# A mixture-of-experts scatter-add that takes the gather's index and bound instead of a row of its own for slots without a token

## The chip, the cores and the metric

The program runs on one core of one Trainium2 chip. The metric is the device time of one execution in microseconds, from the first to the last instruction of that core, lower is better. One launch computes the whole reference; nothing is computed on the host.

## The reference, cut to what matters

The reference is three stages on 512 tokens of width 1024: two hybrid layers (a gated delta rule, attention, a linear recurrence), one layer with differential attention and retention, and at the end of that layer a mixture of experts with 64 experts of which each token uses 8. Only this last part is touched. Cut to its core it is:

```python
scores = sigmoid(h @ router_w)                       # (512, 64)
top_e  = top 8 of the 4 best of 8 groups             # (512, 8)
wts    = scores[top_e] / sum * 2.5
tok_buf = full((n_pad,), t).at[dest].set(t_s)        # slots of experts; an empty slot names row t
h_pad   = concatenate([h, zeros((1, d))])
def body(acc, (tok, wt, e)):                         # blocks of 128 slots of one expert
    xb = h_pad[tok]
    yb = (silu(xb @ w1[e]) * (xb @ w3[e])) @ w2[e]   # 1024 -> 256 -> 1024
    return acc.at[tok].add(yb * wt[:, None])
out = rmsnorm(x + g2 * (acc[:t] + shared(h)))
```

512 tokens with 8 experts each are 4,096 pairs of a token and an expert.

## The kernel before

**Who sets the order.** The kernel does not issue instructions as it is written. Every engine operation is first recorded (`Rec.add`), and a list scheduler (`Rec.plan`) then sorts the whole program, from the first layer to the last expert, by estimated durations and priorities (the longest path to the end). Line 411 issues everything, so all instructions carry that line in the profile, and groups are told apart by tile names. A recorded operation that is left out shifts the ranks of what follows, and the scheduler may then place other operations elsewhere. PE, DVE, ACT, POOL and SP each run their own list strictly in order.

**The mixture of experts** (`block3`). `h2` makes the normalised rows and writes them to a DRAM tensor `h2d`; it also copies the residual into the accumulator `accd` in DRAM. `route` finds for each expert which slot each token takes, and sorts the experts by their number of tokens; the sorted experts get slots by a fixed table:

```python
FIXED = 4
CAPS = (96,) * 4 + (192,) * 4 + (128,) * 5 + (96,) * 11 + (80,) * 11 + (64,) * 7 + (48,) * 14 + (32,) * 8
```

The sum of this table is 5,104 slots for the 4,096 pairs; with the given inputs every expert fits, so 1,008 slots hold no token, and a loop for what overflows (line 2276) runs no iteration. The four experts with 192 slots ("wide experts") are worked off in two blocks, of 128 and of 64 slots; all others are one block. That makes 68 blocks. With these inputs the wide experts hold 183, 145, 132 and 130 tokens, and the last two experts 16 and 12 tokens in 32 slots each.

**One block** (`block`, then `ffn`) does this for its `c` slots:
1. DVE makes a one-hot matrix `oh` (tokens by slots), PE multiplies it with the table `aux` (in the profile a matmul `ps<-aux,b`), DVE sums the result into `m`: the token's number less a large constant `HUGE`, and the weight.
2. DVE turns it into an index, `ix`: with `HUGE` added back a slot with a token has the token's row, a slot without one has 1,048,576.
3. POOL issues a gather (`DMA_INDIRECT raw<-h2d,m`) of `c` rows of 4 KB into the buffer `X`, with a bound: rows past 511 are skipped.
4. PE transposes `X` (eight `ps<-const,raw`), ACT and DVE split half of the result into two fp32r parts, PE multiplies with the expert's weights (`ps<-raw,b` for the quarter in plain fp32, `ps<-b,b` for the rest).
5. DVE scales the result into the buffer `Y` (`SCALAR_TENSOR_TENSOR raw<-ps,m,b`), and POOL issues a scatter (`DMA_INDIRECT accd<-raw,m`) that adds its `c` rows to `accd`. In this kernel the scatter has no bound. Its own index column holds `min(ix, 512 + slot)`: the accumulator has 128 extra rows, set to zero in `shared`, and a slot without a token adds to one of them.

`X` lies in three buffers (`raw4` to `raw6`). `Y` shares four (`raw0` to `raw3`) with the first sixth of each expert's weights, which SP loads (`raw<-in_ew_dram`); SP loads the rest into smaller buffers `b`. A scatter waits for the scatter before it (both write `accd`), and POOL's list is one queue, in which scatters and gathers alternate. The shared expert (`shared`) adds its 512 rows with four more scatters. After the last scatter `tail` reads `accd`, normalises and writes the output.

Of the kernel before, what the change touches and what calls it, by code (L numbers as in the profile page):

```python
# [12 lines left out]
F32 = mybir.dt.float32  # L13
F32R = mybir.dt.float32r
BF16 = mybir.dt.bfloat16
I32 = mybir.dt.int32
U32 = mybir.dt.uint32
AF = mybir.ActivationFunctionType
OP = mybir.AluOpType
AX = mybir.AxisListType  # L20

T = 512
NT = 4
D = 1024
# [1380 lines left out]
HUGE = 1048576.0  # L1405
# [455 lines left out]
class K3(K2):  # L1861
    def h2(self):
        nc = self.nc
        self.acc = self.dr.tile([640, D], F32, name="accd")
        self.h2d = self.dr.tile([T, D], F32, name="h2d")
        G = [self.mrow(4, i) for i in range(2)]
        S = [self.mrow(3, i) for i in range(2)]
        hs = []
        for t in range(NT):
            r = self.rstd1(self.x[t], "h2")  # L1870
            for i in range(2):
                x = self.x[t][i]
                nc.sync.dma_start(self.acc[t * 128:(t + 1) * 128, i * 512:(i + 1) * 512], x)
                nc.vector.scalar_tensor_tensor(x, x, r, G[i], op0=OP.mult, op1=OP.mult)
                o = self.t2()
                pk = lambda a: a.rearrange("q (p k) -> q p k", k=4)
                nc.vector.tensor_tensor(out=o.rearrange("q (k p) -> q p k", k=4), in0=pk(x), in1=pk(S[i]), op=OP.add)
                nc.sync.dma_start(self.h2d[t * 128:(t + 1) * 128, i * 512:(i + 1) * 512], o)
                hs.append(o)
        self.h = []  # L1880
        for k in range(8):
            p = self.psum("tr")
            for t in range(NT):
                self.tr(p[:, t * 128:(t + 1) * 128], hs[2 * t + k // 4][:, (k % 4) * 128:(k % 4 + 1) * 128])
            hi, lo = self.t2(F32R), self.t2(F32R)
            self.split(p, hi, lo)
            self.h.append((hi, lo))

    def route(self):
        nc, A = self.nc, self.A  # L1890
        C = lambda w, n, dt=F32: self.cst.tile([128, w], dt, name=n)
# [73 lines left out]
        ipart, cap, dcap = self.c2[:, 385:386], self.c2[:, 450:451], self.c2[:, 451:452]  # L1965
# [45 lines left out]
        for i in range(3):  # L2011
            d = self.aux[:, :, :, 3 + i]
            nc.vector.tensor_copy(d, s3(rem))
            if i < 2:
                nr = self.t2()[:, :256]
                nc.vector.tensor_tensor(out=s3(nr), in0=s3(rem), in1=d, op=OP.subtract)
                rem = nr
        self.dump_row = C(1, "dumprow")
        nc.vector.tensor_scalar(self.dump_row, ipart, 512.0, None, op0=OP.add)
        pc = self.psum("a")  # L2020
        for t in range(4):
            nc.tensor.matmul(pc[0:64, 0:1], mb[:, 64 * t:64 * t + 64], onesb[:, 0:1], start=(t == 0), stop=(t == 3))
# [35 lines left out]
    def shared(self):  # L2058
        nc, A = self.nc, self.A
        self.g2 = [nc.keep(self.mrow(5, i)) for i in range(2)]  # L2060
        at4 = self.small(4, "at4", I32)
        for t in range(NT):
            nc.vector.tensor_scalar(at4[:, t:t + 1], self.c2[:, 385:386], 128.0 * t, None, op0=OP.add)
        z = self.t2()
        nc.gpsimd.memset(z, 0.0)
        for i in range(2):
            nc.sync.dma_start(self.acc[512:640, i * 512:(i + 1) * 512], z)
        ph = {(i, j): self.psum("mm") for i in range(2) for j in range(2)}
        at = []
        for h in range(2):  # L2070
            for i, n in enumerate(("shared_w1", "shared_w3")):
                nc.gate = at[-SHAHEAD] if len(at) >= SHAHEAD else self.mark - GATE[2]
                w = self.load_w(A[n].rearrange("(h p k) f -> p h k f", h=2, k=4)[:, h], tags=(SHRAW,) + SHTAG)
                nc.gate = None
                at.append(len(nc.ops))
                for k in range(4):
                    hh, hl = self.h[4 * h + k]
                    for j in range(2):
                        wh, wl = (x[:, 128 * j:128 * j + 128] for x in w[k])
                        for q, (a, b) in enumerate(((wh, hh), (wl, hh), (wh, hl))):  # L2080
                            nc.tensor.matmul(ph[i, j], a, b, start=(h + k + q == 0), stop=(h + k + q == 6))
        nc.gate = at[-SHAHEAD2]
        w2 = [self.load_w(A["shared_w2"][j * 128:(j + 1) * 128].rearrange("p (k d) -> p k d", k=2), tags=(SHRAW,) + SHTAG)
              for j in range(2)]
        nc.gate = None
        hs = []
        for j in range(2):
            th, ac, ha = (self.t2() for _ in range(3))
            nc.scalar.activation(th, ph[0, j], AF.Tanh, scale=0.5)
            nc.vector.scalar_tensor_tensor(ac, th, 1.0, ph[0, j], op0=OP.add, op1=OP.mult)  # L2090
            nc.vector.tensor_tensor(out=ha, in0=ac, in1=ph[1, j], op=OP.mult)
            hh, hl = self.t2(F32R), self.t2(F32R)
            nc.scalar.activation(hh, ha, AF.Copy, scale=0.5)
            nc.vector.scalar_tensor_tensor(hl, ha, 0.5, hh.bitcast(F32), op0=OP.mult, op1=OP.subtract)
            hs.append((hh, hl))
        for t in range(NT):
            s = slice(t * 128, (t + 1) * 128)
            y = self.t2(tag=YTAG)
            for n in range(2):
                py = self.psum("mm")  # L2100
                self.mm3(py, [((hs[j][0][:, s], hs[j][1][:, s]), w2[j][n]) for j in range(2)])
                yn = y[:, 512 * n:512 * n + 512]
                nc.scalar.activation(yn, py, AF.Copy)
                nc.gpsimd.tensor_tensor(out=yn, in0=yn, in1=self.g2[n], op=OP.mult)
            nc.gpsimd.indirect_dma_start(out=self.acc[:], out_offset=Ind(at4[:, t:t + 1]), in_=y, in_offset=None,
                                         compute_op=OP.add)
            yield 9.0
# [72 lines left out]
    def block(self, w, pos, aux, c=128):  # L2180
        nc = self.nc
# [5 lines left out]
        for t in range(4):  # L2187
            nc.tensor.matmul(pm, oh[:, t, :], aux(t), start=(t == 0), stop=(t == 3))
        m = self.small(2, "m")[:c]
        nc.vector.tensor_reduce(m, pm.rearrange("p (a b) -> p a b", a=2), axis=AX.X, op=OP.add)  # L2190
        ix = self.small(2, "ix", I32)[:c]
        nc.vector.tensor_scalar(ix[:, 0:1], m[:, 0:1], HUGE, None, op0=OP.add)
        nc.vector.tensor_scalar(ix[:, 1:2], m[:, 0:1], HUGE, self.dump_row[:c], op0=OP.add, op1=OP.min)
        xs = []
        X = self.t2(tag="wr")[:c]
        nc.gpsimd.indirect_dma_start(out=X, out_offset=None, in_=self.h2d[:], in_offset=Ind(ix[:, 0:1]),
                                     bounds_check=T - 1, oob_is_err=False)
        for h in range(2):
            px = self.psum("a")[:, :4 * c]
# [13 lines left out]
        Y = self.t2(tag=YTAG)[:c]  # L2213
        for n in range(2):
            nc.vector.scalar_tensor_tensor(Y[:, 512 * n:512 * n + 512], ys[n], m[:, 1:2], self.g2[n][:c], op0=OP.mult, op1=OP.mult)
        nc.gpsimd.indirect_dma_start(out=self.acc[:], out_offset=Ind(ix[:, 1:2]), in_=Y, in_offset=None, compute_op=OP.add)

    def hold(self, q):
        self.nc.gate = self.seen.get(q, self.mark)
# [144 lines left out]
```

## Time and profile before

| what | value |
|---|---|
| time, median of 3 runs | 2389.94 us (2387.89 to 2395.32) |
| the profiled execution's own time | 2396.73 us |
| its span, first to last instruction | 2395.0 us |
| mean granted TensorE clock | 0.947 |
| PE busy | 2187.3 us (91%) |
| DVE, ACT, POOL busy | 1619.6, 1087.7, 534.6 us |
| expert blocks | from 1574 us to 2377 us of the span |

Times in the rows are microseconds from the span's start. "Busy" is the time in which an engine executes; what it waits for stands as idle time before an instruction with the one that ended it. The clock is the share of full speed (2.4 GHz) that TensorE was granted.

### The profile page before, as it was taken

The page shows a single profiled execution, that of the slowest core. Times are in us where ns is not written, and L with a number is a line of the kernel's source. Part 1 is how long each engine was busy: PE and PEld are TensorE (multiplying, and loading weights), DVE is VectorE, ACT ScalarE, POOL GpSimd, SP SyncE. Part 2 cuts the span into 40 slices and gives each one's busy share as a digit, 9 for nine tenths or more (in the row PEclk, how much of TensorE's full clock was granted, in tenths as well). Part 3 has the DMA queues.
Part 4 walks back from the last instruction along what each step waited for, and adds up shares of the span by engine and source line. Part 5 has one row for each costly group of instructions (what it writes and reads, how often), then busy time and mean ns, then how long its engine had stood idle before and what let it go on. Part 6 is the DMA issues. An engine that isn't in the chain of part 4 may idle for free.

```text
span 2395.0 us, 32613 instructions
## 1 busy us (share of the span) xinstructions
PE 2187.3 (91%) x10382; PEld 1546.5 (65%) x10382; DVE 1619.6 (68%) x3578; ACT 1087.7 (45%) x2272; POOL 534.6 (22%) x393
## 2 busy tenths in 40 slices
PE   6898988999999999999998879879998999999995
PEld 4677866677788877777886657656555555444442
DVE  7995577775695557767733675657676667776775
ACT  5555456453452365445432353335444444544443
POOL 3364334200021010001000132033232233222222
PEclk9998999899999999999998979989999999999998
DMA  5334354223222232314211025349999899999994
GB/s 191 119 102 127 118 172 146 86 84 124 94 78 74 78 116 75 92 63 143 71 54 53 23 66 198 132 116 348 288 341 282 267 294 313 340 334 302 307 311 130
DMA packets 191185, 398.13 MB, mean 166 GB/s; under 512 B 32169, under 2 KB 48297, under 8 KB 191010
## 3 DMA queue, kind: packets, MB, share of 16 engines
q1 hardware_dynamic: 178050, 356.24, 44.1%
q0 software_dynamic: 12960, 39.79, 7.6%
q8 instruction: 82, 1.34, 0.2%
q14 instruction: 93, 0.76, 0.1%
HBM read 358.44 MB, written 41.63 MB: 167 GB/s over the span
## 4 chain that ended last, share of the span: by engine, by line
PE 69%; DVE 13%; DMA 11%; ACT 3%; issue 3%; POOL 1%; SPq 0%; POOLq 0%; DVEq 0%; ACTq 0%
PE ps L411 69%; DVE b L411 10%; DMA raw<-h2d,m 5%; DVE m L411 3%; ACT b L411 3%; DMA accd<-raw,m 1%; DMA raw<-in_adaw_dram 1%; DMA raw<-in_wo_dram 1%; DMA b<-in_ew_dram 1%; POOL raw L411 1%; DMA xdiag<-b 0%; DMA raw<-in_wi_dram 0%; SPq L411 0%; DMA raw<-accd 0%; DMA b<-in_x_dram 0%
## 5 line engine op out<-in xcount | busy, mean ns | idle before, releaser
L411 PE MATMUL ps<-b,b 128*128 128x512 f32 (+9 forms) x8052 | 1870.1, 389 | 83.2 <-DVE b L411 49.6
L411 PEld LDWEIGHTS ps<-b,b 128*128 128x128 f32 (+6 forms) x8052 | 1312.6, 184 | 571.9 <-issue 130.1
L411 ACT ACTIVATE b<-ps 128x512 f32<-128x512 f32 (+16 forms) x661 | 271.1, 431 | 676.6 <-PE ps L411 599.6
L411 DVE TENSOR_TENSOR b<-b,b 128x512 fp32r<-128x512 f32 (+5 forms) x751 | 469.8, 664 | 35.2 <-ACT b L411 18.3
L411 ACT ACTIVATE b<-b 128x512 fp32r<-128x512 f32 (+3 forms) x702 | 393.8, 619 | 121.6 <-DVE b L411 84.5
L411 DVE TENSOR_TENSOR b<-raw,b 128x512 fp32r<-128x512 f32 (+2 forms) x340 | 240.0, 720 | 187.2 <-ACT b L411 173.7
L411 ACT ACTIVATE b<-raw 128x512 fp32r<-128x512 f32 (+3 forms) x348 | 207.2, 611 | 350.3 <-PE ps L411 256.0
L411 POOL DMA_INDIRECT accd<-raw,m x72 | 133.2, 1850 | 367.6 <-DVE raw L411 224.3
L411 PE MATMUL ps<-const,b 128*128 128x128 f32 (+5 forms) x898 | 159.5, 292 | 52.1 <-DVE b L411 39.0
L411 PEld LDWEIGHTS ps<-const,b 128*128 128x128 f32 (+5 forms) x898 | 115.0, 153 | 102.0 <-DVE b L411 49.4
L411 POOL TENSOR_TENSOR raw<-raw,raw 128x1024 f32<-128x1024 f32 x56 | 140.2, 2512 | 159.9 <-ACT raw L411 132.3
L411 PE MATMUL ps<-raw,b 128*96 128x512 f32 (+5 forms) x272 | 151.8, 676 | 5.3 <-ACT raw L411 2.9
L411 POOL DMA_INDIRECT raw<-h2d,m x68 | 100.9, 1483 | 231.0 <-PE ps L411 83.7
L411 DVE SCALAR_TENSOR_TENSOR raw<-ps,m,b 96x512 f32<-96x512 f32 (+5 forms) x136 | 97.5, 740 | 50.9 <-DMA accd<-raw,m 30.1
L411 DVE SCALAR_TENSOR_TENSOR b<-b,ps 128x512 f32<-128x512 f32 (+6 forms) x106 | 54.1, 510 | 102.7 <-ACT b L411 99.2
L411 POOL TENSOR_TENSOR m<-m,mhalf 128x1 f32<-128x1 f32 (+2 forms) x54 | 52.2, 968 | 301.6 <-DVE m L411 301.6
L411 DVE TENSOR_REDUCE m<-ps 128x1 f32<-128x256 f32 (+9 forms) x196 | 75.1, 393 | 60.5 <-PE ps L411 59.0
L411 DVE TENSOR_TENSOR b<-b,ps 128x512 f32<-128x512 f32 (+6 forms) x150 | 82.6, 559 | 49.2 <-PE ps L411 48.5
L411 DVE TENSOR_TENSOR b<-ps,b 128x512 fp32r<-128x512 f32 (+8 forms) x136 | 74.0, 545 | 47.1 <-ACT b L411 38.9
L411 POOL MEMSET b<- 64x512 f32 (+4 forms) x19 | 8.4, 454 | 398.1 <-PE ps L411 326.6
L411 DVE SCALAR_TENSOR_TENSOR b<-ps,cols,b 128x511 f32<-128x511 f32 (+3 forms) x118 | 86.9, 742 | 7.8 <-ACT b L411 6.9
L411 PE MATMUL ps<-const,raw 96*128 96x96 f32 (+5 forms) x544 | 61.0, 249 | 33.4 <-DMA raw<-h2d,m 30.4
(139 smaller groups left out, 1199.0 us busy)
## 6 DMA issues: line engine op xcount, KB each, us to landing
b<-in_ew_dram SPq DMA_DIRECT2D x640, 256.0 KB
raw<-in_wi_dram SPq DMA_DIRECT2D x100, 512.0 KB
raw<-in_ew_dram SPq DMA_DIRECT2D x64, 512.0 KB
raw<-in_adaw_dram SPq DMA_DIRECT2D x48, 512.0 KB
raw<-in_wo_dram SPq DMA_DIRECT2D x40, 512.0 KB
raw<-in_wuq_dram SPq DMA_DIRECT2D x24, 192.0 KB
b<-in_x_dram SPq DMA_DIRECT2D x16, 256.0 KB
zd<-b SPq DMA_DIRECT2D x16, 256.0 KB
```

The source lines that it names most:

```text
L411: getattr(getattr(nc, o.eng), o.fn)(*[real(x) for x in o.a], **{m: real(x) for m, x in o.k.items()})
```

## The change

The accumulator loses its 128 extra rows, the operation that prepares their row numbers (`dump_row`), the zero tile and the two DMAs that clear them. In each block the index is one column in place of two, so one DVE operation goes, and the scatter takes the gather's index and the gather's bound: the rows of slots without a token are skipped.

```diff
-        self.acc = self.dr.tile([640, D], F32, name="accd")
+        self.acc = self.dr.tile([T, D], F32, name="accd")
...
-        self.dump_row = C(1, "dumprow")
-        nc.vector.tensor_scalar(self.dump_row, ipart, 512.0, None, op0=OP.add)
...
-        z = self.t2()
-        nc.gpsimd.memset(z, 0.0)
-        for i in range(2):
-            nc.sync.dma_start(self.acc[512:640, i * 512:(i + 1) * 512], z)
...
-        ix = self.small(2, "ix", I32)[:c]
-        nc.vector.tensor_scalar(ix[:, 0:1], m[:, 0:1], HUGE, None, op0=OP.add)
-        nc.vector.tensor_scalar(ix[:, 1:2], m[:, 0:1], HUGE, self.dump_row[:c], op0=OP.add, op1=OP.min)
+        ix = self.small(1, "ix", I32)[:c]
+        nc.vector.tensor_scalar(ix, m[:, 0:1], HUGE, None, op0=OP.add)
...
-        nc.gpsimd.indirect_dma_start(out=X, out_offset=None, in_=self.h2d[:], in_offset=Ind(ix[:, 0:1]),
+        nc.gpsimd.indirect_dma_start(out=X, out_offset=None, in_=self.h2d[:], in_offset=Ind(ix),
                                      bounds_check=T - 1, oob_is_err=False)
...
-        nc.gpsimd.indirect_dma_start(out=self.acc[:], out_offset=Ind(ix[:, 1:2]), in_=Y, in_offset=None, compute_op=OP.add)
+        nc.gpsimd.indirect_dma_start(out=self.acc[:], out_offset=Ind(ix), in_=Y, in_offset=None,
+                                     bounds_check=T - 1, oob_is_err=False, compute_op=OP.add)
```

The scheduler, with these operations gone, also orders other work differently. The lists are the same up to the first expert blocks and nearly the same again from the 32nd block on; between them blocks move against each other. Three places follow; in them `x2` or `x4` counts equal instructions in a row, and a line of "..." stands for rows left out.

On PE, at the block behind the first half of the second wide expert: `aux` is the block's one-hot matmul (its buffer names the block), `const,raw` are transposes of gathered rows, 128x64 those of a wide expert's second block. Before, from the block's last one-hot matmul to its transposes (`raw_151`), the first "..." holds three one-hot matmuls of another block and the second twelve expert matmuls of 96 rows:

```order
L411 MATMUL ps_69<-aux,b_14955 96x6
L411 MATMUL ps_70<-const_152,b_15047 128x96 x2
L411 MATMUL ps_71<-const_152,raw_149 128x64 x2
...
L411 MATMUL ps_72<-const_152,raw_150 128x96 x4
...
L411 MATMUL ps_71<-const_152,raw_149 128x64 x4
L411 MATMUL ps_72<-const_152,raw_151 128x96 x4
```

In the changed kernel the same block (`b_14958`, its rows in `raw_149`) has the twelve matmuls, then two plain fp32 ones and fourteen more, in the "...":

```order
L411 MATMUL ps_70<-aux,b_14958 96x6
L411 MATMUL ps_69<-const_152,b_15051 128x96 x2
L411 MATMUL ps_71<-const_152,raw_151 128x64 x2
L411 MATMUL ps_72<-const_152,raw_150 128x96 x4
...
L411 MATMUL ps_67<-raw_146,b_15069 96x512 x2
...
L411 MATMUL ps_71<-const_152,raw_149 128x96 x4
```

So sixteen more matmuls now stand between this block's one-hot and its transposes, and the same holds at the third wide expert.

On PE two expert blocks later: before, the one-hot of the block `b_15230` is followed by two plain fp32 matmuls, two transposes, 24 and more expert matmuls and then the block's transposes. In the changed kernel (`b_15228`, rows in `raw_149`) the "..." holds ten expert matmuls of 96 rows in the first place, and one-hot matmuls that repeat in the others:

```order
L411 MATMUL ps_70<-aux,b_15228 96x6
L411 MATMUL ps_68<-b_15378,b_15453 96x512
...
L411 MATMUL ps_69<-aux,b_15002 64x6
...
L411 MATMUL ps_70<-aux,b_15345 128x6
...
L411 MATMUL ps_71<-const_152,raw_149 128x96 x4
```

Here the one-hot moved to eleven expert matmuls ahead of its transposes.

On SP, among the weight loads into the buffers that `Y` shares, from the tenth to the thirteenth (with what each waits for; `DMASW` are POOL's gathers and scatters, `DMAHW` SP's own loads, a line of "..." holds loads into `b`). Before:

```order
L411 DMA raw3_148<-in_ew_dram 128x1024 [waits DMAHW3_49,PE_49]
...
L411 DMA raw2_147<-in_ew_dram 128x1024 [waits DMAHW0_49,PE_49]
...
L411 DMA raw0_145<-in_ew_dram 128x1024 [waits DMAHW5_49,DMASW6_49]
...
L411 DMA raw3_148<-in_ew_dram 128x1024 [waits DMAHW4_49,PE_49]
```

Now:

```order
L411 DMA raw3_148<-in_ew_dram 128x1024 [waits DMAHW1_49,PE_49]
...
L411 DMA raw1_146<-in_ew_dram 128x1024 [waits DMASW3_49,DMAHW0_49,DMASW1_49,DVE_49]
...
L411 DMA raw2_147<-in_ew_dram 128x1024 [waits DMAHW7_49,PE_49]
...
L411 DMA raw0_145<-in_ew_dram 128x1024 [waits DMASW7_49,DMAHW6_49,DMASW5_49,DVE_49]
```

Two of these four loads now wait for scatters, one did before; over all 65 such loads 17 wait for a scatter now and 11 before.

## Rows read from the trace of the kernel before

**Rows 1.** The page: busy time, share of the span, instructions of each engine.

```profile
PE 2187.3 (91%) x10382; PEld 1546.5 (65%) x10382; DVE 1619.6 (68%) x3578; ACT 1087.7 (45%) x2272; POOL 534.6 (22%) x393
```

**Rows 2.** Stretches: length, busy PE, PEld, DVE, ACT, POOL, clock, DMA share, GB/s.

```profile
1600.00:2340.00 740.00, 696.82 (x2960) 366.30 (x2959) 524.90 (x1130) 345.56 (x747) 220.57 (x132) 0.96 0.97 308
1806.00:1812.80 6.80, 4.18 (x9) 1.98 (x10) 1.31 (x5) 2.56 (x5) 1.52 (x2) 0.50 0.63 154
1891.30:1898.10 6.80, 6.27 (x13) 2.60 (x12) 1.49 (x2) 0.95 (x2) 0.91 (x1) 0.50 0.68 193
1966.40:1973.20 6.80, 5.50 (x12) 2.81 (x13) 5.29 (x14) 0.88 (x2) 3.99 (x2) 0.50 0.66 165
2040.00:2100.00 60.00, 57.85 (x258) 27.93 (x257) 44.75 (x100) 29.19 (x66) 17.78 (x11) 1.00 1.05 344
```

**Rows 3.** Waits from 1600 to 2340 us: total, times, longest.

```profile
PE ps L411 <- DMA raw<-h2d,m: 30.4, 15, 4.7
DVE raw L411 <- DMA accd<-raw,m: 30.1, 13, 5.3
POOL raw L411 <- DMA accd<-raw,m: 18.1, 3, 7.1
PEld ps L411 <- DMA b<-in_ew_dram: 6.9, 23, 0.3
```

**Rows 4.** PE's timeline around the block b_14955 (1796 to 1812 us).

```profile
1799.30 0.30 PE L411 MATMUL ps<-aux,b 128*96 128x6 bf16 x4
...
1800.54 3.00 PE L411 MATMUL ps<-b,b 128*96 128x512 f32 x12
1803.47 0.46 PE L411 MATMUL ps<-const,raw 64*128 64x64 f32 x4
1808.62 0.87 PE L411 MATMUL ps<-const,raw 96*128 96x96 f32 x4 [4.69 <-DMA raw<-h2d,m]
...
1809.57 2.87 PE L411 MATMUL ps<-raw,b 128*96 128x512 f32 x3
```

**Rows 5.** PE's timeline at the other two long waits for a gather.

```profile
1716.48 0.30 PE L411 MATMUL ps<-aux,b 128*96 128x6 bf16 x4
...
1725.40 1.51 PE L411 MATMUL ps<-const,raw 96*128 96x96 f32 x8 [4.18 <-DMA raw<-h2d,m]
...
1882.36 0.28 PE L411 MATMUL ps<-aux,b 128*80 128x6 bf16 x4
...
1890.90 0.47 PE L411 MATMUL ps<-const,raw 80*128 80x80 f32 x4 [4.07 <-DMA raw<-h2d,m]
```

**Rows 6.** The page: DMA queues, packets, MB, share of 16 engines.

```profile
q1 hardware_dynamic: 178050, 356.24, 44.1%
q0 software_dynamic: 12960, 39.79, 7.6%
```

**Rows 7.** The chain that ended last: scatters on it (start, us).

```profile
1579.69 6.13 DMA accd<-raw,m
...
2008.10 10.57 DMA accd<-raw,m
...
2368.84 3.78 DMA accd<-raw,m
...
2373.35 3.59 DMA accd<-raw,m
```

**Rows 8.** The indirect DMAs on POOL: duration in ns, minimum, median, maximum.

```profile
L411 POOL DMA_INDIRECT accd<-raw,m x72: 1330/1590/4037, 1579.7 to 2373.4; - x72
...
L411 POOL DMA_INDIRECT raw<-h2d,m x68: 935/1024/5811, 1574.5 to 2350.6; - x68
```

**Rows 9.** The DVE operations that go (ns, minimum, median, maximum).

```profile
L411 DVE TENSOR_SCALAR m<-m,dumprow x68: 190/200/206, 1574.1 to 2349.8; 96x1 int32<-96x1 f32 x15, 48x1 int32<-48x1 f32 x14, 64x1 int32<-64x1 f32 x11, 80x1 int32<-80x1 f32 x11
```

**Rows 10.** POOL's timeline where the zero tile is made.

```profile
1457.11 0.53 POOL L411 MEMSET b<- 128x512 f32 x1 [8.71 <-DVE m L411]
```

**Rows 11.** SP's waits for scatters from 1605 to 2340 us: total, times, longest.

```profile
SPq L411 <- DMA accd<-raw,m: 37.4, 7, 7.3
```

## The prediction

> **What bounds the kernel now.** I read the page first: PE is busy for 91% of the span [rows 1], so a change that only shortens another engine or a transfer earns what PE waits for it. All expert work lies behind 1574 us, so next come the stretches: from 1600 to 2340 us PE is busy for 696.8 of 740 us, and the DMA engines are busy too, share 0.97 at 308 GB/s, over 1 in a good stretch [rows 2]. Two resources are near their limit, and PE has 43.2 us idle. The waits say for what: 30.4 us in 15 waits of PE are for gathered rows [rows 3], no other releaser of PE comes near, and weights cost it 6.9 us in pieces of at most 0.3 us.
>
> The timeline shows how such a wait arises. At 1799.60 us the last one-hot matmul of a block ends (1799.30 + 0.30); its rows are there for the transposes at 1808.62, 9.0 us later, through DVE's reduction and index, POOL and the gather. PE has 4.3 us of work ahead of them (to 1803.93) and waits 4.69 [rows 4]. At 1716.78 and 1882.64 it is the same: 8.6 and 8.3 us later, waits of 4.18 and 4.07 [rows 5]. So a block whose one-hot stands 9 us of PE work ahead of its transposes waits for nothing; these three, 12.94 us of the 30.4, stand closer. A wait is paid twice: after the last two of them and after 1966 us the granted clock is 0.50, which is 1.2 GHz, for 6.8 us, with PE busy for 4.18, 6.27 and 5.50 us in it [rows 2]. At full speed half of that would do, so a fall costs 2.1 to 3.1 us; I take 2.6.
>
> **The change part by part.** Sums are made on the profiled execution (2396.73 us, span 2395.0), which lies 6.8 us over the median of 2389.94; the difference is then applied to the median.
>
> *Rows left out.* The table has 5,104 slots for 4,096 pairs. The queue of POOL moved 39.79 MB [rows 6]; 4,096 gathered rows and 5,104 + 512 scattered ones of 4,096 B are 39.78 MB. So a bound does leave out the bytes, and 1,008 scattered rows go. Their packets do not: 5,104 + 5,616 + 16 for each of 140 DMAs are 12,960, the number in the row, so a skipped row stays as a small packet. What does a row cost? Work of the queue: 7.6% of 16 engines for 2395 us, 2,912 us, over 9,712 rows with data is 300 ns a row if both kinds cost the same; if a gathered row goes at the rate of the other queue (44.1%, 16,899 us for 356.24 MB: 194 ns for 4 KB), a scattered one is 377 ns. 1,008 rows are then 18.9 to 23.8 us of all 16 engines. On the path a row counts by the landing: 128 rows took 6.13 us and 32 rows 3.78 in quiet stretches [rows 7], 24.5 ns a row over a fixed 3.0 us. In traffic 80 rows took 10.57, which gives at most 95 ns. A mean block drops 14.8 rows: 0.36 us in quiet, at most 1.4 us in traffic; I take 0.5, near the quiet end, since part of the 10.57 us is the 4 us that an instruction on POOL can take [rows 8].
>
> The Trainium skill, page "DMA: Bandwidth & Descriptors", section "Anatomy of one DMA — SWDGE (gpsimd) path", speaks against this part: a DMA of POOL has a fixed cost of about 2 us, mostly the receipt, and its bytes move at 436 GB/s. By that figure, an estimate, the 36 rows of the last two scatters would be 0.34 us. This case's rows agree on a large fixed part (3.0 us), but their slope is 2.6 times as steep.
>
> Where does it reach PE? (a) The end: the last two scatters run one behind the other on the chain [rows 7], and with 16 and 12 tokens in 32 slots they drop 36 rows: 0.9 us. (b) Gathers: POOL's list alternates scatter and gather in one queue, so a gather issued right behind a scatter lands after it. Without the three long waits 17.5 us in 12 waits remain [rows 3]; I let half of them have a scatter directly ahead: 6 x 0.5 = 3 us (none: 0; all at 1.4: 16.8). (c) DVE waits 30.1 us for a scatter to free `Y`, POOL 18.1 us [rows 3]. This is hidden behind PE's own work and counts nothing; without that cover 16 waits x 0.5 would be 8 us.
>
> *One DVE operation less a block.* 68 of 200 ns, 13.6 us [rows 9]. DVE is busy for 524.9 of 740 us, and the operation stands behind the index that the gather takes. Mostly hidden behind PE: 1 us (bounds 0 and 13.6).
>
> *Zero tile, its two DMAs, `dump_row`.* 0.53 us on POOL after 8.71 us of idleness [rows 10], one operation on DVE, two short issues on SP, all 100 us before the first scatter: nothing; without that cover, under 2 us.
>
> *The bound on POOL.* The trace has no bounded scatter. The bounded gather takes 1,024 ns in the median, the unbounded scatter 1,590 [rows 8]. If the bound makes a scatter as quick as a gather, the 6 gathers behind one start 0.57 us sooner, if it costs as much again, later: 3.4 us either way, taken as nothing.
>
> *What the scheduler moves.* This is the largest term. The block at 1799.30 gets sixteen more matmuls between its one-hot and its transposes. Twelve expert matmuls take 3.00 us there and a plain fp32 one 0.96 (2.87 for three) [rows 4]: two plain and fourteen others are 5.4 us. Added to its 4.3, less 0.46 us for the four transposes that no longer stand there, PE has 9.2 us of work where 9.0 are needed, and the wait of 4.69 goes. The third wide expert's block has the same order, so the 4.07 go. The 4.18 at the first wide expert stays, one block later. Against this, `b_15228` now has its one-hot eleven expert matmuls (2.75 us) and some 0.5 us of other one-hots ahead of its transposes: 8.6 - 3.25 = 5.4 us of new waiting. Net -4.69 - 4.07 + 5.4 = -3.4 us, and one fall of the clock fewer, -2.6: -6.0 us (bounds: +5.4 + 2.6 = +8 if only the new wait comes, -14 if it does not).
>
> Sum: -0.9 - 3 - 1 - 6.0 = -10.9, so 11 us: 2385.7 for the profiled execution, **2379 us** for the median.
>
> **The rivals.**
>
> *No change.* What is freed turns up as the next wait: PE is busy for 94% of the stage, the landing is mostly fixed, skipped rows keep their packets, and a gather that comes early is followed by one that does not. Only the end's 0.9 us stay: 2389, range 2385 to 2393. For it: the 30.1 us of DVE's waits that PE hardly feels; against it: the long waits hang on the order of PE's list, which is known.
>
> *The DMA engines are the bound.* With a share of 0.97 to 1.05 [rows 2] all 18.9 to 23.8 us of engine time come off: 2366 to 2371. Against it: PE waits 6.9 us in all for weights.
>
> *Slower: weight loads behind scatters.* Of 65 loads into the buffers that `Y` shares 17 now wait for a scatter, 11 before, and SP's list is in order, so all loads behind are late. Before, seven such waits, up to 7.3 us, 37.4 in all [rows 11], never reached PE by more than 0.3 us at a time [rows 3]. If two of the new ones follow each other within a block, 14.6 us meet a cover of some 7.3, and PE waits 7.3 us and 2.6 for the clock: 10 us. One such place cancels the forecast; from two on the kernel is slower: 2379 + 20 = 2399.
>
> **How the numbers follow.** About 0.3%, 7 us, is what a measurement of this kernel can tell from no change. Chances: forecast 0.45 (own range 2371 to 2386; 0.38 of it more than 7 us faster, 0.07 within), no change 0.24 (0.22 the same, 0.02 faster), DMA bound 0.14 (faster), loads behind scatters 0.17 (0.14 slower, 0.03 the same). Faster 0.54, same 0.32, slower 0.14. The range 2366 to 2398 takes in the first three and of the last the places that stop short of two: about 0.85. The bounds of single terms (POOL 3.4, order +8 and -14) lie inside it.
>
> **What the profile afterwards would show.** Bytes of the software queue: 39.79 - 4.13 = 35.66 MB, packets still 12,960. No wait of over 1 us for gathered rows beside the second and third wide expert, one of about 4 at the first, a new one of about 5.4 us with the clock at 0.50 behind it, ahead of the last wide expert; PE's waits for gathers 24 us in place of 30.4. The last two scatters on the chain at about 3.4 and 3.1 us. A bounded scatter between 1.0 and 1.6 us on POOL. The prediction is wrong if PE waits for weights for more than 0.3 us at a time, if the one-hot of `b_15228` costs no wait, or if the second half, where the order is the same, gains or loses more than 5 us.

## The result, and the profile after

The changed kernel takes 2411.35 us in the median of 6 runs (2409.7 to 2416.04), the kernel before 2390.71 (2387.89 to 2395.32): a ratio of 1.0086, 95% interval 1.0071 to 1.01. Forecast were 2379 us and a range of 2366 to 2398. The change costs 0.9%.

The page of the changed kernel, engines (busy time, share of the span, instructions) and POOL's queue (packets, MB, share of 16 engines), against [rows 1, 6]:

```profile
PE 2187.6 (91%) x10382; PEld 1543.0 (64%) x10382; DVE 1613.4 (67%) x3509; ACT 1086.9 (45%) x2272; POOL 572.6 (24%) x392
...
q0 software_dynamic: 12960, 35.67, 6.7%
```

The bytes fell as the change says (39.79 to 35.67 MB), the packets did not. DVE has 6 us less to do, and POOL, from which the change takes one instruction, is busy for 38 us more. Its indirect DMAs in the changed kernel, against [rows 8] (ns: minimum, median, maximum; first and last start):

```profile
L411 POOL DMA_INDIRECT accd<-raw,m x72: 1313/1636/4054, 1576.8 to 2389.2; - x72
...
L411 POOL DMA_INDIRECT raw<-h2d,m x68: 937/1056/5697, 1571.5 to 2366.5; - x68
```

The last column also measures the expert stage: from the first gather's start to the last scatter's it is 817.7 us, and 798.9 in [rows 8]. That is 18.8 us more. The span grew by 15.8, since the first gather came 3.0 us sooner; over all runs of this document the stage starts between 1565.6 and 1578.9 us, so these 3.0 us say nothing of the change. Cut at the same blocks (the 18th and the 9th scatter from the end, at 2187.37 and 2303.60 us after, 2194.04 and 2292.04 before), the stage lasts 615.9 us up to the first cut (before: 619.6), 116.2 between the cuts (98.0) and 85.6 behind them (81.3). Nearly all of the loss, 18.2 us, lies between the cuts. The nine gathers there are those of the last seven blocks of 48 slots and the first two of 32, and the lists of all engines are nearly those of before there but for the removed operation.

Between the cuts, first the changed kernel, then the kernel before (length; busy PE, PEld, DVE, ACT, POOL; granted clock; DMA share; GB/s):

```profile
2187.37:2303.60 116.23, 103.84 (x415) 44.80 (x414) 71.09 (x156) 48.42 (x110) 51.44 (x19) 0.90 0.83 264
```

```profile
2194.04:2292.04 98.00, 95.52 (x413) 42.55 (x412) 71.75 (x163) 48.08 (x108) 25.23 (x19) 0.97 0.97 317
```

POOL is busy for 51 us in place of 25 with as many instructions, PE idles for 12.4 us in place of 2.5, its clock falls from 0.97 to 0.90, and the DMA engines move less in a microsecond. POOL's timeline of the changed kernel shows which instructions became long:

```profile
2187.37 1.37 POOL L411 DMA_INDIRECT accd<-raw,m  x1 [8.38 <-DVE raw L411]
2189.04 4.09 POOL L411 DMA_INDIRECT raw<-h2d,m  x1 [0.30 <-PE ps L411]
2197.70 1.37 POOL L411 DMA_INDIRECT accd<-raw,m  x1 [4.56 <-DVE raw L411]
2202.47 4.54 POOL L411 DMA_INDIRECT raw<-h2d,m  x1 [3.41 <-issue]
```

and of the kernel before at the same blocks:

```profile
2194.04 1.37 POOL L411 DMA_INDIRECT accd<-raw,m  x1 [8.54 <-DVE raw L411]
2195.72 1.07 POOL L411 DMA_INDIRECT raw<-h2d,m  x1 [0.30 <-PE ps L411]
2204.35 1.36 POOL L411 DMA_INDIRECT accd<-raw,m  x1 [7.57 <-DVE raw L411]
2206.02 1.09 POOL L411 DMA_INDIRECT raw<-h2d,m  x1 [0.30 <-PE ps L411]
```

The scatters, which got the bound, take 1.37 us in both. The gathers, which the change leaves alone, take 4.1 and 4.5 us in place of 1.1. All nine between the cuts take 3.9 to 4.5 us after; before, one of nine does (4.02 us) and the others take 1.0 to 1.5. What DVE does at that moment, before:

```profile
2195.61 0.34 DVE L411 TENSOR_TENSOR b<-const2t,posm 128x192 bf16<-128x192 f32 x1
2195.87 0.20 DVE L411 TENSOR_SCALAR m<-m,dumprow 48x1 int32<-48x1 f32 x1
2196.00 3.08 DVE L411 TENSOR_TENSOR b<-b,b 128x512 fp32r<-128x512 f32 x5
```

and after:

```profile
2188.93 0.34 DVE L411 TENSOR_TENSOR b<-const2t,posm 128x192 bf16<-128x192 f32 x1
2189.20 3.08 DVE L411 TENSOR_TENSOR b<-b,b 128x512 fp32r<-128x512 f32 x5
```

The operation that is gone stood between the next block's one-hot comparison (`b<-const2t,posm`) and a run of five subtractions (`b<-b,b`) that make the low parts of expert weights. Before, the comparison ends at 2195.95 us and the run starts at 2196.00, 0.05 us behind it; the gather, which started at 2195.72, ends at 2196.79, 0.84 us after the comparison's end. After, the run starts at 2189.20, 0.07 us ahead of the comparison's end (2189.27); the gather, which started at 2189.04, ends at 2193.13, 0.85 us after the run's end (2192.28). So the run comes 0.13 us sooner, and the gather gets in behind the run and not behind the comparison.

How far the gather starts ahead of the run does not decide it alone. The next gather of the changed kernel (2202.47, above) starts 0.6 us ahead of its run and takes 4.54 us; a gather of the kernel before, at the fourth of the nine blocks, starts 0.7 us ahead of its run and takes 1.53:

```profile
2202.82 0.34 DVE L411 TENSOR_TENSOR b<-const2t,posm 128x192 bf16<-128x192 f32 x1
2203.09 3.08 DVE L411 TENSOR_TENSOR b<-b,b 128x512 fp32r<-128x512 f32 x5
```

```profile
2229.32 1.53 POOL L411 DMA_INDIRECT raw<-h2d,m  x1 [2.98 <-issue]
...
2229.66 0.34 DVE L411 TENSOR_TENSOR b<-const2t,posm 128x192 bf16<-128x192 f32 x1
2229.93 0.20 DVE L411 TENSOR_SCALAR m<-m,dumprow 48x1 int32<-48x1 f32 x1
2230.06 3.08 DVE L411 TENSOR_TENSOR b<-b,b 128x512 fp32r<-128x512 f32 x5
```

At the comparison's end the run has begun in the one (0.07 us ago) and not in the other (0.06 us to go). The first gather ends 0.84 us after the run, the second 0.85 us after the comparison. The one slow gather of the kernel before between the cuts started at 2216.53, only 0.04 us ahead of the comparison's end and 0.1 ahead of the run, and took 4.02.

PE feels it like this in the changed kernel (waits in brackets):

```profile
2199.35 1.09 PE L411 MATMUL ps<-const,raw 48*128 48x48 f32 x8 [2.92 <-DMA raw<-h2d,m]
...
2224.98 0.69 PE L411 MATMUL ps<-const,raw 48*128 48x48 f32 x8 [2.02 <-DMA raw<-h2d,m]
...
2250.28 1.08 PE L411 MATMUL ps<-const,raw 48*128 48x48 f32 x8 [2.61 <-DMA raw<-h2d,m]
...
2276.91 0.75 PE L411 MATMUL ps<-const,raw 48*128 48x48 f32 x8 [2.73 <-DMA raw<-h2d,m]
```

Between the cuts PE waits 12.3 us for gathered rows (six waits), before 2.5 (one): 9.8 us. And it is busy for 103.8 us in place of 95.5 with two matmuls more, at the lower clock: 8.3 us. Together 18.1 of the 18.2.

### The profile page after: what moved, and what is told of

Read it like the earlier page. It is cut to its first block, busy times and chain, and to the rows that moved or that the text cites. A ratio compares the mean times of both kernels' runs of the same rounds, so it can differ in the third digit from the quotient of the medians.

```text
span 2410.8 us, 32650 instructions
## 1 busy us (share of the span) xinstructions
PE 2187.6 (91%) x10382; PEld 1543.0 (64%) x10382; DVE 1613.4 (67%) x3509; ACT 1086.9 (45%) x2272; POOL 572.6 (24%) x392
## 3 DMA queue, kind: packets, MB, share of 16 engines
q0 software_dynamic: 12960, 35.67, 6.7%
## 5 line engine op out<-in xcount | busy, mean ns | idle before, releaser
L411 POOL DMA_INDIRECT accd<-raw,m x72 | 144.0, 2000 | 373.5 <-DVE raw L411 210.9
L411 POOL DMA_INDIRECT raw<-h2d,m x68 | 127.5, 1875 | 206.5 <-PE ps L411 80.7
L411 PE MATMUL ps<-const,raw 48*128 48x48 f32 (+5 forms) x544 | 61.9, 252 | 37.7 <-DMA raw<-h2d,m 35.9
```

The costliest lines, as they stand in the source:

```text
L411: getattr(getattr(nc, o.eng), o.fn)(*[real(x) for x in o.a], **{m: real(x) for m, x in o.k.items()})
```

## The experiments

The theory: the removed operation kept DVE's run of subtractions out of the gather's way on POOL, and its 0.13 us are worth 18 us. The expectations call it the window theory in runs 1 to 4 (the gather gets in while the operation runs) and the **head-start** theory from run 5 on (the gather has to start some 0.2 us ahead of the run). Rivals: the new order costs (**order**); the bound or the skipped rows cost (**bound**); and, within the theory, whether the kind of the removed operation matters or its time. The table gives every run; a ratio is to executions of the kernel before taken along with that run, so it can differ from the quotient of the medians shown; "stage" and "part" are the stage and the part between the cuts in the profiled execution, in us, "slow" the gathers over 1.8 us in that part (XAHEAD moves gathers across the cuts, so their number differs).

| run | median us | ratio to before, interval | stage | part | slow |
|---|---|---|---|---|---|
| before | 2390.71 | | 798.9 | 98.0 | 1 of 9 |
| changed | 2411.35 | 1.0086 (1.0071 to 1.01) | 817.7 | 116.2 | 9 of 9 |
| bound alone, order of before | 2389.85 | 0.9992 (0.9976 to 1.0009) | 797.1 | 95.2 | 1 of 9 |
| the same, operation gone | 2407.37 | 1.0072 (1.0051 to 1.0093) | 817.0 | 117.7 | 9 of 9 |
| changed, operation put back | 2391.13 | 1.0005 (0.9988 to 1.0022) | 798.7 | 94.8 | 1 of 9 |
| changed, another operation as long | 2389.82 | 0.9988 (0.9971 to 1.0005) | 801.4 | 97.9 | 1 of 9 |
| changed, three operations | 2400.83 | 1.002 (1.0003 to 1.0036) | 801.6 | 93.5 | 0 of 9 |
| operation gone but in 48-slot blocks | 2396.68 | 1.001 (0.9993 to 1.0028) | 800.5 | 104.4 | 3 of 9 |
| changed, XAHEAD 9 | 2405.74 | 1.005 (1.0033 to 1.0068) | 811.0 | 84.4 | 2 of 6 |
| changed, XAHEAD 12 | 2385.26 | 0.9972 (0.9954 to 0.9989) | 793.1 | 96.5 | 4 of 6 |
| changed, one SBUF input | 2367.76 | 0.9898 (0.9871 to 0.9925) | 763.7 | 93.4 | 0 of 9 |
| XAHEAD 12, operation put back | 2388.74 | 0.9976 (0.9958 to 0.9994) | 789.8 | 95.0 | 4 of 6 |
| changed, XAHEAD 18 | 2382.37 | 0.9951 (0.9934 to 0.9968) | 783.7 | 93.6 | 2 of 7 |
| before, XAHEAD 18 | 2390.57 | 1.0007 (0.9984 to 1.003) | 800.4 | 101.9 | 6 of 6 |

**1. The bound alone.**

```diff
-        nc.vector.tensor_scalar(self.dump_row, ipart, 512.0, None, op0=OP.add)
+        nc.vector.tensor_scalar(self.dump_row, ipart, 4.0 * HUGE, None, op0=OP.add)
...
-        nc.gpsimd.indirect_dma_start(out=self.acc[:], out_offset=Ind(ix[:, 1:2]), in_=Y, in_offset=None, compute_op=OP.add)
+        nc.gpsimd.indirect_dma_start(out=self.acc[:T], out_offset=Ind(ix[:, 1:2]), in_=Y, in_offset=None,
+                                     bounds_check=T - 1, oob_is_err=False, compute_op=OP.add)
```

> Before with the bound on the scatter alone: the dump row's constant becomes 4 x 2^20, so that the minimum leaves the gather's index, and the scatter gets the bound; both index operations, the zero tile and the order of every engine stay as before. Rows of empty slots are left out of the scatter. Window theory (the loss comes from the removed DVE operation): no loss here, 2385 to 2391 us, the gathers after 2190 us at about 1.0 us on POOL. Rival 'the bound or the skipped rows cost': about 2405 to 2411. Rival 'the new order costs': 2385 to 2391 as well.

2389.85 us, no difference. POOL's queue moves 35.67 MB here too, and the bounded scatters take 1,580 ns in the median (1,590 in [rows 8]). The rival "bound" falls: 1,008 rows fewer, with nothing else changed, are worth nothing that can be measured.

**2. The operation gone, too.** The operation is planned as before and then not issued, so the lists differ in its 68 places alone; the scatter takes the gather's index (last line):

```diff
         for o in order:
+            if o in self.gone:
+                continue
...
         nc.vector.tensor_scalar(ix[:, 1:2], m[:, 0:1], HUGE, self.dump_row[:c], op0=OP.add, op1=OP.min)
+        nc.gone.add(nc.ops[-1])
...
+        nc.ops[-1].k["out_offset"] = Ind(ix[:, 0:1])
```

> The first run's kernel, and the second index operation (m<-m,dumprow, 200 ns on DVE, 68 times) is not issued; every engine's order is otherwise that of before. Window theory: gathers of the 48-row blocks (about 2190 to 2300 us) take 4 us on POOL instead of 1, PE waits 2 to 3 us for most of them with the clock falling behind, 2405 to 2412 us. Rivals 'order' and 'bound': no different from the first run.

2407.37 us, and the gathers as in the changed kernel (POOL, from the first cut on):

```profile
2180.80 1.37 POOL L414 DMA_INDIRECT accd<-raw,m  x1 [8.54 <-DVE raw L414]
2182.48 4.09 POOL L414 DMA_INDIRECT raw<-h2d,m  x1 [0.30 <-PE ps L414]
2191.10 1.37 POOL L414 DMA_INDIRECT accd<-raw,m  x1 [4.54 <-DVE raw L414]
2195.75 4.54 POOL L414 DMA_INDIRECT raw<-h2d,m  x1 [3.28 <-issue]
```

In the order of before, leaving out 68 operations of 200 ns makes the kernel 0.8% slower than run 1, and the part between the cuts as long as in the changed kernel. The rival "order" is not needed.

**3 and 4. Something put back in the changed kernel.** Behind the next one-hot comparison on DVE one operation is issued that no one uses, once a TENSOR_SCALAR of one column, once a TENSOR_TENSOR of 60 columns (the lines that set up `index` and the unused tile `junk` are left out):

```diff
+            if o in self.index:
+                owed.append(self.index[o])
+            if o.eng == "vector" and owed and o.k.get("op") == OP.is_equal:
+                for junk, slots, c2, c in owed:
+                    nc.vector.tensor_scalar(junk[:c, 0:1], slots[:c, 0:1], HUGE, c2[:c, 385:386], op0=OP.add, op1=OP.min)
+                owed = []
```

> The changed kernel in its own order, with a TENSOR_SCALAR of one column (as long as the removed one, on constants, into an unused tile) put on DVE behind each next one-hot comparison. Window theory: gathers back at about 1 us, 2383 to 2391 us, and what it gains on the first run is what the new order is worth (about 4 us). Rival 'the new order costs': 2408 or more. Rival 'bound': 2408 or more.

```diff
-                    nc.vector.tensor_scalar(junk[:c, 0:1], slots[:c, 0:1], HUGE, c2[:c, 385:386], op0=OP.add, op1=OP.min)
+                    nc.vector.tensor_tensor(out=junk[:c, 0:60], in0=slots[:c, 0:60], in1=slots[:c, 0:60], op=OP.add)
```

> As the third run, but the operation put in is a TENSOR_TENSOR of 60 columns with both inputs in SBUF, about as long (some 0.2 us). Window theory, in its form that DVE operations with two SBUF inputs keep the gather's instruction from getting on: no window, 2407 to 2415 us. Rival 'only the 200 ns of delay matter, whatever fills them': as the third run, 2383 to 2391.

2391.13 and 2389.82 us. POOL in the first of the two:

```profile
2195.11 1.06 POOL L413 DMA_INDIRECT raw<-h2d,m  x1 [0.30 <-PE ps L413]
...
2205.58 4.02 POOL L413 DMA_INDIRECT raw<-h2d,m  x1 [0.30 <-PE ps L413]
...
2217.33 1.53 POOL L413 DMA_INDIRECT raw<-h2d,m  x1 [1.93 <-issue]
```

An operation without use takes the loss away: after one slow gather the rhythm comes back by itself, as before. That a TENSOR_TENSOR does it as well was not expected: what counts of the removed operation is the time by which it put off the run. Why this one, whose inputs lie in SBUF too, does not hold the gather itself is not shown. And run 3 against run 1 is the new order (and the missing zero tile): 2391.13 to 2389.85, nothing that can be measured.

The traces of both kernels and of runs 1 to 6 show what decides between the cuts. Without the operation the run starts 0.07 us ahead of the comparison's end, and all 20 such gathers are slow. With it, or with another in its place, the run starts at least 0.05 us behind that end, and 47 of 52 are quick; the five slow ones all started less than 0.05 us ahead of the comparison's end and 0.09 to 0.10 us ahead of the run. Six of the nine slow gathers of the changed kernel started 0.49 to 0.61 us ahead of the run, so it is the window, and not the head start, that the removed operation gave.

**5. Three operations in place of one.**

```diff
-                    nc.vector.tensor_scalar(junk[:c, 0:1], slots[:c, 0:1], HUGE, c2[:c, 385:386], op0=OP.add, op1=OP.min)
+                    for i in range(3):
+                        nc.vector.tensor_scalar(junk[:c, i:i + 1], slots[:c, 0:1], HUGE, c2[:c, 385:386], op0=OP.add, op1=OP.min)
```

> As the run with one operation put back, with three of them one behind the other on DVE behind each next one-hot comparison (some 0.4 us more head start for the gather than in the changed kernel, 0.13 us each). Head-start theory (a gather that starts on POOL at least 0.2 us ahead of DVE's run of 128x512 subtractions takes 1 us, one that starts later waits for the run's end): no gather of the 48-row blocks over 1.8 us, the single slow ones at about 0.1 us of head start go too; 2380 to 2390 us. Rival: 0.4 us of DVE a block cost more than they bring, 2393 to 2400.

2400.83 us, a miss. Between the cuts it did what was expected (no slow gather, 93.5 us), but behind them gathers of the other blocks of 32 slots are slow:

```profile
2303.60 3.59 POOL L413 DMA_INDIRECT raw<-h2d,m  x1 [1.10 <-issue]
...
2316.57 3.08 POOL L413 DMA_INDIRECT raw<-h2d,m  x1 [0.31 <-issue]
2328.66 3.06 POOL L413 DMA_INDIRECT raw<-h2d,m  x1 [0.30 <-PE ps L413]
```

Behind the cut the stage takes 91.1 us, in place of 87.0 in run 3. The delay that helps in one kind of block can put the gather into a run in another. This does not account for the miss: the whole stage is only 2.9 us longer than in run 3, the medians lie 9.7 us apart, and what makes up the rest is not shown.

**6. The operation gone everywhere but in the 48-slot blocks.** Run 2's kernel with one condition:

```diff
-        nc.gone.add(nc.ops[-1])
+        if c != 48:
+            nc.gone.add(nc.ops[-1])
```

> The kernel with the second index operation gone and the order of before, but the 14 blocks of 48 rows keep it; the other 54 blocks are without it. Head-start theory: the loss sits in the 48-row blocks alone, 2387 to 2393 us. Rival 'the operation matters in every block': in between, about 2400 to 2404.

2396.68 us, 1.001 with an interval from 0.9993: little of run 2's loss is left. The expectation put the loss into the 48-slot blocks alone, and that is not quite so. Of the three slow gathers one is that of run 1, and the other two, at 2267.04 and 2280.96 us, are those of the first two blocks of 32 slots, which have lost their operation; the part between the cuts is 9.2 us longer than in run 1. Ahead of the first cut, where all but the 48-slot blocks have lost it too, nothing is lost: 612.6 us, and 616.7 in run 1.

**7, 8, 10, 11 and 12. More work of PE ahead of the transposes.** If late gathers cost only what PE feels of them, a block whose one-hot stands a block earlier should not mind. `XAHEAD` (6 in both kernels) lets the planner do that; no other line changes, but the order does, from the first expert on.

```diff
-XAHEAD = 6
+XAHEAD = 9
```

> The changed kernel with XAHEAD 9 in place of 6: the planner may place a block's one-hot matmuls up to a third of an expert... three steps of the expert before earlier; in the order that comes out, the blocks of 48 rows have 15.8 us of PE work between one-hot and transposes in place of 7.6. No operation is put back, so the gathers stay slow where they start late. Head-start theory: a gather of 4 us is then hidden, PE waits under 10 us in all for gathered rows, 2370 to 2390 us. Rival 'the buffers that rows now hold longer make weight loads late': PE waits for weights, 2400 or more.

> As the run before with XAHEAD 12: most 48-row blocks have 15.8 us too, the last ones 8.5. Head-start theory: 2372 to 2392 us. Rival as there.

> XAHEAD 12 (which came out at 0.9972 of the kernel before) with the small operation put back behind each next one-hot comparison. Head-start theory: the gathers that are slow there too become fast where their blocks have only 8.5 us of PE work, 2375 to 2386 us. Rival: one-hots that stand a block earlier have taken what there was to gain, the operation only costs, 2384 to 2392.

> The changed kernel with XAHEAD 18: nearly every block has 17 us or more of PE work between its one-hot and its transposes. If only the gathers' lateness counts, PE waits for gathered rows nearly vanish and it is the fastest: 2360 to 2378 us. If what the run with XAHEAD 9 showed (slower with more cover) is a cost of planning ahead (row buffers held longer, weight loads and DVE work pushed behind), it is slower than before: 2395 to 2415.

> The kernel before with XAHEAD 18: both index operations, the dump row, all rows scattered. If the change costs only what PE feels of late gathers, it costs nothing where every block has 17 us of cover: the same as the changed kernel with XAHEAD 18 (0.9951 of the kernel before), 2378 to 2388 us, or 1 to 2 us above it for the scattered rows. Rival: the operation helps there as well, 2365 to 2375.

XAHEAD 9 was a miss (2405.74): its order brings the one-hots of the last blocks of 32 slots closer to their transposes (down to 6.7 us of PE's work, 7.5 or more in the changed kernel), PE waits there for up to 5.27 us at a time, and behind the second cut the stage takes 105.0 us in place of 81.3. XAHEAD 12 gave 2385.26, and the operation put back adds nothing to it (2388.74). XAHEAD 18 gave 2382.37, between the two ranges expected, and faster than the kernel before by 0.5% and, by the medians, than the changed one by 1.2%. PE's waits in it from 1600 to 2340 us:

```profile
PE ps L411 <- DVE b L411: 16.9, 6, 6.2
PE ps L411 <- DVE raw L411: 16.9, 5, 8.9
...
PE ps L411 <- DMA raw<-h2d,m: 3.2, 2, 1.7
```

The waits for gathered rows, 30.4 us in [rows 3], are gone, and 33.8 us of waits for DVE stand in their place (4.2 in the kernel before). With the operation and all rows kept, XAHEAD 18 is no gain (2390.57), and all six gathers between its cuts are slow: an expectation missed on both sides. With this setting the change gains (the intervals of the two runs lie apart), but their orders differ throughout, so the pair doesn't say what of it brings that.

**9. What of DVE's run holds the gather.** Each subtraction of the weights' split reads two SBUF tensors. Here it is replaced by an operation of the same shape that reads one (512 times in the trace, not 544 as the expectation says; the low parts of the weights are left out):

```diff
             self.split(self.raw[p], hi, lo)
+            nc.single.add(nc.ops[-1])
...
+            if o in self.single:
+                nc.vector.tensor_scalar(out=real(o.k["out"]), in0=real(o.k["in1"]), scalar1=2.0 ** -12, scalar2=0.0,
+                                        op0=OP.mult, op1=OP.add, accum_out=self.junk)
```

> The changed kernel in its own order; the 544 VectorE subtractions that make the low parts of the expert weights (TENSOR_TENSOR, two SBUF inputs) are each replaced by a TENSOR_SCALAR with accumulation that reads one SBUF input (the high part times 2^-12), so the low parts of the weights are not computed. Theory that two SBUF inputs on VectorE hold up the gather's instruction: the run of five no longer holds it, no gather of the 48-row blocks over 1.8 us though they start as late as in the changed kernel, no PE wait of 2 to 3 us there, stage shorter by 15 us or more (2375 to 2397 us). Rival 'any long run of VectorE holds it': gathers of 4 us as before, 2405 to 2420.

2367.76 us, below the expected range. DVE's timeline around a gather that starts on POOL at 2066.69 us, and that gather:

```profile
2066.49 0.69 DVE L410 TENSOR_SCALAR_CACHE_REDUCE b<-b 128x512 fp32r<-128x512 f32 x1 [0.23 <-ACT b L415]
2067.10 0.08 DVE L410 DVE_READ_ACCUMULATOR b<-b 128x1 f32 x1
2067.29 0.69 DVE L410 TENSOR_SCALAR_CACHE_REDUCE b<-b 128x512 fp32r<-128x512 f32 x1
```

```profile
2066.69 0.99 POOL L415 DMA_INDIRECT raw<-h2d,m  x1 [0.30 <-issue]
```

It starts 0.20 us into an operation of 0.69 and is done 0.50 us after that operation's end; the held gathers above needed 0.84 or 0.85. All indirect DMAs of this run:

```profile
L415 POOL DMA_INDIRECT accd<-raw,m x72: 1313/1434/1943, 1574.6 to 2333.1; - x72
...
L415 POOL DMA_INDIRECT raw<-h2d,m x68: 937/998/1404, 1569.4 to 2309.9; - x68
```

No gather takes over 1.41 us, though DVE is no less busy (0.69 us an operation against 0.68, and 0.08 for the accumulator). Between the cuts few gathers of this run meet such an operation, so the whole stage has to be counted. Ten gathers start 0.06 us or more into one, with at least 0.15 us of it to go, and take 0.95 to 1.02 us. In the two kernels 36 start like that into a two-input subtraction and take 1.02 to 5.81 us, and 34 of these end 0.82 to 0.91 us after the end of a subtraction. So it is not any long operation of DVE that holds POOL's gathers, but this subtraction; the replacement differs from it by its one input and also by its kind, so that the second input does it is likely, and not shown by itself. The stage of the profiled execution is 54 us shorter than in the changed kernel, but that execution was 11 us quicker than the median of its run; by the medians the run is 44 us below the changed kernel and 23 below the kernel before. That suggests that the kernel before pays for held gathers too, in other places (its PE waits 30.4 us for gathered rows, here 13.2); no run separates it.

## Why the prediction was wrong

**The step that failed** is "One DVE operation less a block": "Mostly hidden behind PE: 1 us (bounds 0 and 13.6)". I counted the operation as 200 ns of DVE's time and let removing it gain or do nothing; I did not ask what stands next to it on another engine. It was a spacer of 0.13 us that let DVE's one-hot comparison end before the run of subtractions began, and POOL's gather get in between. Without it the gather has to wait for the run's end in nine blocks of nine (before in one), lasts 3 us longer, the 9.5 us that PE has to do between a block's one-hot and its transposes (2186.93 to 2196.43 us) no longer suffice, it waits 1.8 to 2.9 us in five of the nine blocks, and its clock falls. Runs 2, 3 and 4 show it both ways: gone from the old order the loss is there, put back into the new one it is not. The slow gathers were in [rows 8] (5,811 ns beside a median of 1,024); I used them for a scatter's price and not as a wait with a cause.

**The term for the order**, -6.0 us, measured nothing (run 3 against run 1, 1.3 us the other way in the median, inside the intervals). Its places were right: in the changed kernel no wait of PE for a gather stands at the second and third wide expert, and the new one does, 6.38 us where 5.4 were forecast; the one at the first is 1.80 us where about 4 were. Other waits there took the gain back:

```profile
1729.26 1.54 PE L411 MATMUL ps<-const,raw 96*128 96x96 f32 x8 [1.80 <-DMA raw<-h2d,m]
...
1797.78 2.55 PE L411 MATMUL ps<-b,b 128*96 128x512 f32 x10 [2.62 <-DVE m L411]
1841.50 1.54 PE L411 MATMUL ps<-const,raw 96*128 96x96 f32 x8 [6.38 <-DMA raw<-h2d,m]
...
1881.16 2.55 PE L411 MATMUL ps<-b,b 128*96 128x512 f32 x10 [1.02 <-DVE m L411]
```

At 1797.78 and 1881.16 the work that moved behind the wide experts' one-hots now waits for DVE, and the clock was 0.50 for 10.2 us from 1837 on, not 6.8. Up to the first cut PE idles 37.8 us of 580 (from 1600), before 38.8 of 587: one microsecond of the six.

**The rows left out**, -3 and -0.9 us. The bytes (35.67 MB, forecast 35.66) and the packets were as forecast. The end gained 0.36 us: the last two scatters on the chain that ended last take 3.62 and 3.39 us, against 3.78 and 3.59 in [rows 7].

```profile
2384.83 3.62 DMA accd<-raw,m
...
2389.18 3.39 DMA accd<-raw,m
```

With 16 and 20 rows fewer that is about 10 ns a row, not 24.5; the slope came from a 128-row scatter at the stage's start and doesn't hold for the skipped rows of small ones, whose packets stay. The prediction's other estimate, 0.34 us for the 36 rows, came closer. That gathers behind scatters come sooner is not to be seen: run 1, where nothing but the rows changes, has a ratio of 0.9992, 2 us, with an interval that takes in no change.

**Costed at nothing and right:** the bound on POOL, the zero tile and its DMAs.

**The slower rival**, weight loads behind scatters, was the wrong mechanism. PE waits 8.5 us for weights in 27 waits, the longest 0.6, against 6.9 and 0.3 in [rows 3]: 1.6 us. Two of the forecast's three signs of being wrong did fire: PE's longest wait for weights is 0.6 us and not 0.3, and the second half, with the order of before, lost far more than 5 us. Only the second has to do with the loss.

**What stays open:** why these gathers are held through a whole run, while others are let in between two operations of one; how early a gather must start for the window to serve it; and what makes the change a gain with XAHEAD 18.

## What to carry to other kernels

Before taking an operation out of a list, look at what starts on the other engines while it runs: an operation of 200 ns that nobody waits for can make the gap in which another engine gets its turn. An instruction whose longest time is five times its median has a cause, and it is worth finding before predicting anything that moves it. A repeating pattern multiplies a small shift: nine blocks in a row lost 2 us each to a shift of 0.13 us.

## What the runs showed of the hardware

- A gather of POOL can be held by DVE's one-hot comparison or 128x512 subtractions, which read two SBUF tensors each; it then ends 0.83 to 0.85 us after the end of the comparison or of the run of subtractions (between the cuts, in both kernels and all runs up to the sixth). It needs a window: with at least 0.05 us from the comparison's end to the run's start it takes 1.0 to 1.5 us in 47 of 52 cases, with the run started 0.07 us ahead of that end 3.9 to 4.5 us in 20 of 20. The Trainium skill, page "SBUF — State Buffer", section "Who interferes with whom", says that a DVE instruction with two SBUF inputs contends with a GpSimd instruction that reads SBUF, and that one with at most one SBUF input does not, outside the faster modes in which it uses two ports. The runs agree for the 128x512 operations: 4.09 us in the changed kernel against 0.99 in run 9. Run 4's addition of 60 columns, which reads one SBUF tensor twice, held no gather; that stays unexplained. The same section says that a probe did not show `tensor_tensor` stalling a DMA, and infers as the reason that writing a DMA's descriptors needs only the write side; here an indirect DMA, whose index lies in SBUF, takes 4.09 us in place of 1.07, and the measurement decides.
- Not every gather next to such a run is held. In the changed kernel one starts 0.03 us into a run of three such subtractions and takes 0.94 us:

```profile
2165.26 1.95 DVE L411 TENSOR_TENSOR b<-b,b 128x512 fp32r<-128x512 f32 x3 [0.26 <-ACT b L411]
...
2165.29 0.94 POOL L411 DMA_INDIRECT raw<-h2d,m  x1 [12.26 <-PE ps L411]
```

- The hold mostly lasts for the whole run of back-to-back operations (3.08 us for five), but not always: of the 34 gathers counted under run 9, nine were let in between two operations of a run. The kernel before has this one, done 0.4 us ahead of the run's end:

```profile
2349.88 2.48 DVE L411 TENSOR_TENSOR b<-b,b 128x512 fp32r<-128x512 f32 x4
...
2350.55 1.43 POOL L411 DMA_INDIRECT raw<-h2d,m  x1 [0.30 <-issue]
```

- The stage's start lies at 1565.6 to 1578.9 us over these runs, though what stands ahead of it is the same or nearly so; a difference of 5 us between single executions says nothing, and the stage has to be measured from its own start.
